# Expert outputs summed in DRAM by accumulating transfers, and another order in the 64-row seats of a mixture of experts

## The chip, the cores and the metric

The kernel runs on one core of a Trainium2 chip, as one program with one launch. The metric is the device time of that launch in microseconds (us), the median of several runs; less is better. Five engines work side by side, each through its own list of instructions: PE (TensorE, matmuls), DVE (VectorE), ACT (ScalarE), POOL (GpSimd) and SP (SyncE, which here only issues transfers). They meet at semaphores.

## The reference

A network of two blocks of layers (gated linear recurrences, attention, convolutional and gated feed-forward layers) over 256 tokens of width 1024 in float32. Only the last layer is touched, a mixture of eight experts of hidden width 3584, two to a token:

```
logits = t @ w_router                        # t: 256 x 1024
top_vals, top_idx = lax.top_k(logits, 2)
gates = softmax(top_vals)
combine = sum(one_hot(top_idx, 8) * gates[..., None], axis=1)
for e in range(8):
    he = (silu(t @ w_gate[e]) * (t @ w_up[e])) @ w_down[e]
    out = out + combine[:, e:e + 1] * he
return rmsnorm(h + out, final_norm)
```

## The kernel before

**Weights.** Every float32 weight matrix comes from DRAM once, in transfers of 1 MB on SP's queue, and each is cut in two pieces of 128 x 1024. ACT writes a rounded copy `hi` of a piece, DVE the rest `lo` (`weights`, `split`, L390 and L391), and PE multiplies with both. Raw weights have twelve buffers in the experts' stage, and `hi` and `lo` four each. A transfer into a raw buffer waits until DVE has read what was in it.

**Seats.** The router (`route`) ranks the experts by how many tokens they got. The rank decides the seat: seats 0, 2, 4 and 6 have 128 rows, seats 1, 3, 5 and 7 have 64. A token row is gathered into a seat by a matmul with a matrix of zeros and ones, `pe` (`expert_picks`, L1804; `expert_gather`), after which ACT and DVE copy the result from PSUM into `xg` (128 rows) or `xgs` (64 rows). In a 128-row seat each product is three matmuls (hi by hi, hi by lo, lo by hi). In a 64-row seat the hi and lo halves of the 64 rows stand side by side in one operand of 128 columns, a product is two matmuls, and the two halves are added afterwards by a matmul with the constant `fold`. One piece of such a seat's up weights, the last, isn't split: PE multiplies it in float32 as it is (`raw`).

**A chunk.** A seat is seven chunks of 512 hidden units (`expert_ffn`). In each PE does the gate product (two 1 MB weights, result `acc`), the up product (two more), and then the down product of the chunk before (`downs`, two weights `w_md`, result `g`). ACT applies Silu to the gate (L1917), DVE multiplies by the up half (L1918, `hc`), PE transposes `hc` into the PSUM tile `pt`, and ACT and DVE write it back as `th`; the next chunk's `downs` need `th`. In a 64-row seat ACT first copies the gate sum (`both`, L1911) and PE folds it.

**Between seats.** At the end of a seat `expert_gate` scales its output by the token's gate on DVE (L1944) and splits it into `y`, hi on ACT and lo on DVE. In chunk 0 of the next seat `expert_scatter` spreads the rows over the 256 tokens by eight matmuls with the transposed `pet`, and DVE adds the four results to the residual `x` (L1957). Seats 1, 3 and 5 also gather the rows of the two next seats, one quarter in each of chunks 2 to 5, and their `pet` and gates in chunk 6 (`hooks`). In `route` the names of the experts and the gates are computed by small DVE instructions (L1755 to L1782) ahead of the first `pe`.

The order of instructions on each engine is that in which the program is written, but where `issue_after` puts one behind another.

Of the kernel before, what the change touches and what calls it, by code (L numbers as in the profile page):

```python
# [21 lines left out]
P = 128  # L22
T = 256
# [11 lines left out]
HALF = P // 2  # L35
PLACE = (0, 4, 1, 5, 2, 6, 3, 7)
# [66 lines left out]
def layout(I):  # L103
# [52 lines left out]
    cst.add("tie", np.tile(np.array([1.0e6] + [-float(e) for e in range(1, 8)], np.float32), (P, 1)))  # L156
    cst.add("fold", (ar[:, None] % HALF == ar[None, :] % HALF).astype(np.float32))
# [83 lines left out]
class Net:  # L241
# [69 lines left out]
    def mm(self, out, lhsT, rhs, start, stop):  # L311
        return self.nc.tensor.matmul(out, lhsT, rhs, start=start, stop=stop)  # L312

    def weights(self, view, raw=None, whole=()):
# [19 lines left out]
        for q in range(pieces):  # L334
# [7 lines left out]
            with ExitStack() as held:  # L342
                if self.hold:
                    for ins in self.hold.pop(0):
                        held.enter_context(self.tc.issue_after(ins))
                self.last_lo = self.split(hi, lo, src)
# [1332 lines left out]
    def route(self, gp, lg, ss, hh, hl, xo):  # L1679
# [33 lines left out]
        with self.tc.issue_after(self.routed.ins):  # L1713
            who, most = self.names(gp, mk, seats, ps[:, 2, :])
            comb = self.gates(mk, S, ss, m, oh1, oh2)
            combp = mk("cp", [P, 2, 8, 2])
            self.seated(gp, seats, combp[:, :, :, 0], comb[:, :, :, 0])
            nc.vector.tensor_copy(combp[:, :, :, 1], comb[:, :, :, 1])
        return hh, hl, xo, posp, combp, (pos, comb, rank, who, most)

    def ranked(self, gp, mk, cnt):
# [10 lines left out]
        seats = self.tl(gp, "seats", S, bufs=1)  # L1732
# [14 lines left out]
    def names(self, gp, mk, seats, cnt):  # L1747
# [5 lines left out]
        who = self.tl(self.rt, "rtwho", [P, 8], I32)  # L1753
        most = self.tl(self.rt, "rtmost", [P, 1], I32)
# [11 lines left out]
        return who, most  # L1766

    def gates(self, mk, S, ss, m, oh1, oh2):
# [9 lines left out]
        comb = mk("cb", [P, 2, 8, 2])  # L1778
# [4 lines left out]
        return comb  # L1783
# [23 lines left out]
    def expert_gather(self, picks, r, q):  # L1807
        nc = self.nc
        pe, xg, kinds = picks
        for part, src in enumerate(r[:2]):  # L1810
            ps = self.tl(self.ps_m, "m", [P, 2, 2, P])
            for c in range(2):
# [5 lines left out]
            for e, small in enumerate(kinds):  # L1818
                if small:
                    sl = slice(HALF * part, HALF * part + HALF)  # L1820
                    dst, src_ = xg[e][:, 2 * q : 2 * q + 2, sl], ps[:, :, e, sl]
                else:
                    dst, src_ = xg[e][:, part, 2 * q : 2 * q + 2, :], ps[:, :, e, :]
                if part == 0:
                    nc.scalar.activation(dst, src_, AF.Copy)
                else:
                    nc.vector.tensor_copy(dst, src_)

    def expert_spread(self, mp, picks, e0, comb):
# [3 lines left out]
        for e in range(len(picks[2])):  # L1833
            ps = self.tl(self.ps_m, "m", [P, 3, P])
            for t in range(2):
                nc.tensor.transpose(ps[:, t, :], pef[:, t, e, :], self.ident)
            for t in range(2):
                self.mm(ps[:, 2, 0:2], pef[:, t, e, :], comb[:, t, e0 + e, :], t == 0, t == 1)
            pet = self.tl(mp, "pet", [P, 2, P], F32R, bufs=4)
            gs = self.tl(mp, "gs", [P, 2], bufs=4)  # L1840
            nc.scalar.activation(pet, ps[:, 0:2, :], AF.Copy)
            nc.vector.tensor_copy(gs, ps[:, 2, 0:2])
            out.append((picks[1][e], pet, gs))
# [9 lines left out]
    def expert_ffn(self, mp, small, first, e, xg, gs, hooks, final):  # L1853
# [5 lines left out]
        def downs(c):  # L1859
            ht = hts.pop(c)  # L1860
            for q in range(2):
                w = self.weights(i["w_md"][e, 2 * c + q])
# [24 lines left out]
        for c in range(7):  # L1887
            gu = []
            for t in range(2):
                ps = self.tl(self.ps_acc, "acc", [P, 512])  # L1890
                for kh in range(2):
# [16 lines left out]
                    if small and (t, kh) == (1, 0):  # L1908
                        both = self.tl(mp, "both", [P, 512], bufs=1)
                        with after(self.last_hi.ins):  # L1910
                            nc.scalar.activation(both, gu[0], AF.Copy)  # L1911
                gu.append(ps)
            if small:
                self.mm(gu[0], self.c("fold"), both, True, True)
            hc = self.tl(mp, "hc", [P, 512])
            with after(self.last_hi.ins):
# [32 lines left out]
    def expert_scatter(self, mp, y, pet, xo, ss=None):  # L1949
        nc = self.nc  # L1950
        for n in range(2):
            for t in range(2):
# [9 lines left out]
    def experts(self, mp, r, out):  # L1962
# [3 lines left out]
        pend = None  # L1966
# [3 lines left out]
        def fetch(e0):  # L1970
            picks = self.expert_picks(mp, e0, r[3], (False, True))
            steps = [lambda q=q: self.expert_gather(picks, r, q) for q in range(4)]
# [144 lines left out]
```

## Time and profile before

| | us |
|---|---|
| median of 3 runs (2133.77 to 2135.83) | 2134.26 |
| the profiled execution | 2133.42 |
| its span, first to last instruction | 2131.6 |
| PE busy in the span | 2025.5 |
| DVE busy | 1771.0 |
| ACT busy | 1389.2 |
| POOL busy | 119.6 |

The profiled execution's time is 1.8 us more than its span. An engine is busy while it executes; register, branch and semaphore instructions don't count, and ends of matmuls are modelled, so that neighbouring matmuls overlap in the rows and their starts tell more than their lengths. The experts begin at about 1143 us and last to the end. Chunks below run from one Silu (L1917) to the next.

### The profile page before, as it was taken

The page shows a single profiled execution, that of the slowest core. Times are in us where ns is not written, and L with a number is a line of the kernel's source. Part 1 is how long each engine was busy: PE and PEld are TensorE (multiplying, and loading weights), DVE is VectorE, ACT ScalarE, POOL GpSimd, SP SyncE. Part 2 cuts the span into 40 slices and gives each one's busy share as a digit, 9 for nine tenths or more (in the row PEclk, how much of TensorE's full clock was granted, in tenths as well). Part 3 has the DMA queues.
Part 4 walks back from the last instruction along what each step waited for, and adds up shares of the span by engine and source line. Part 5 has one row for each costly group of instructions (what it writes and reads, how often), then busy time and mean ns, then how long its engine had stood idle before and what let it go on. Part 6 is the DMA issues. An engine that isn't in the chain of part 4 may idle for free.

```text
span 2131.6 us, 34865 instructions
## 1 busy us (share of the span) xinstructions
PE 2025.5 (95%) x13159; PEld 1744.7 (82%) x13159; DVE 1771.0 (83%) x2896; ACT 1389.2 (65%) x1950; POOL 119.6 (6%) x178
## 2 busy tenths in 40 slices
PE   9999999999999899999887999999989999999997
PEld 8889998889999789999887877778666876678764
DVE  7788888659897679886866989898889988898887
ACT  7566565456556575445535878878777777778785
POOL 1000001002120001222200000000000000000000
PEclk9999999999999999999998999999999999999999
DMA  6335544333654344556564999999999999999992
GB/s 242 131 123 203 178 160 159 104 135 135 219 201 166 87 161 175 210 215 220 204 243 159 360 357 378 396 355 379 342 353 368 368 364 337 360 369 367 349 390 114
DMA packets 80336, 540.13 MB, mean 253 GB/s; under 512 B 9216, under 2 KB 10592, under 8 KB 18208
## 3 DMA queue, kind: packets, MB, share of 16 engines
q1 hardware_dynamic: 76080, 523.59, 65.9%
q0 software_dynamic: 4080, 14.24, 1.8%
q8 instruction: 105, 1.72, 0.3%
q14 instruction: 71, 0.58, 0.1%
HBM read 527.74 MB, written 10.06 MB: 252 GB/s over the span
## 4 chain that ended last, share of the span: by engine, by line
PE 78%; DVE 14%; DMA 3%; issue 2%; ACT 2%; SPq 0%; DVEq 0%; ACTq 0%
PE acc L312 37%; PE g L312 36%; DVE lo L391 6%; PE m L312 4%; DMA raw<-w_me 1%; ACT hi L390 1%; DMA raw<-w_md 1%; PE m L1930 1%; DVE xz L1539 1%; DVE hc L859 1%; PE m L934 0%; DVE y L391 0%; ACT U L1488 0%; PE m L1436 0%; DVE hc L1944 0%
## 5 line engine op out<-in xcount | busy, mean ns | idle before, releaser
L391 DVE TENSOR_TENSOR lo<-raw,hi 128x1024 fp32r<-128x1024 f32 (+1 forms) x956 | 1128.6, 1215 | 185.3 <-ACT hi L390 175.9
L390 ACT ACTIVATE hi<-raw 128x1024 fp32r<-128x1024 f32 (+1 forms) x956 | 983.6, 1051 | 323.7 <-PE g L312 196.9
L312 PE MATMUL g<-xh,hi 128*128 128x256 f32 (+1 forms) x1612 | 462.0, 287 | 14.9 <-ACT xh L467 9.2
L312 PE MATMUL g<-xl,hi 128*128 128x256 f32 (+1 forms) x1612 | 460.8, 286 | 0.8 <-DVE xl L471 0.7
L312 PE MATMUL g<-xh,lo 128*128 128x256 f32 (+1 forms) x1612 | 457.6, 284 | 2.1 <-DVE lo L391 2.1
L312 PEld LDWEIGHTS g<-xh,hi 128*128 128x128 f32 (+1 forms) x1612 | 308.2, 192 | 19.5 <-ACT xh L467 10.8
L312 PEld LDWEIGHTS g<-xh,lo 128*128 128x128 f32 (+1 forms) x1612 | 308.7, 192 | 4.2 <-DVE lo L391 3.4
L312 PEld LDWEIGHTS g<-xl,hi 128*128 128x128 f32 (+1 forms) x1612 | 308.9, 192 | 3.1 <-DVE xl L471 1.5
L312 PE MATMUL acc<-hi,xg 128*128 128x512 f32 x896 | 283.0, 392 | 0.0
L312 PE MATMUL acc<-lo,xgs 128*128 128x512 f32 x392 | 176.5, 450 | 25.4 <-DVE lo L391 24.7
L312 PEld LDWEIGHTS acc<-hi,xg 128*128 128x128 f32 x896 | 168.1, 188 | 35.0
L312 PE MATMUL acc<-lo,xg 128*128 128x512 f32 x448 | 176.3, 394 | 1.8 <-DVE lo L391 1.8
L312 PE MATMUL g<-lo,th 128*128 128x512 f32 x448 | 167.9, 409 | 1.2 <-DVE lo L391 1.2
L312 PE MATMUL g<-hi,th 128*128 128x512 f32 x448 | 159.9, 415 | 1.2 <-ACT th L390 1.2
L312 PE MATMUL acc<-hi,xgs 128*128 128x512 f32 x392 | 154.1, 397 | 0.0
L312 PE MATMUL acc<-ah,lo 128*128 128x256 f32 x528 | 148.0, 281 | 1.4 <-DVE lo L391 1.4
L312 PE MATMUL acc<-al,hi 128*128 128x256 f32 x528 | 148.6, 282 | 0.0
L312 PE MATMUL acc<-ah,hi 128*128 128x256 f32 x528 | 147.2, 282 | 0.0
L312 PEld LDWEIGHTS acc<-lo,xgs 128*128 128x128 f32 x392 | 73.5, 188 | 84.0 <-DVE lo L391 66.9
L312 PEld LDWEIGHTS g<-hi,th 128*128 128x128 f32 x448 | 84.4, 188 | 29.4 <-issue 5.5
L312 PEld LDWEIGHTS acc<-lo,xg 128*128 128x128 f32 x448 | 84.2, 188 | 23.5 <-DVE lo L391 6.2
L312 PEld LDWEIGHTS g<-lo,th 128*128 128x128 f32 x448 | 79.7, 188 | 28.4 <-DVE lo L391 14.2
(512 smaller groups left out, 3019.5 us busy)
## 6 DMA issues: line engine op xcount, KB each, us to landing
raw<-w_me SPq DMA_DIRECT2D x223, 1024.0 KB, 7.0
raw<-w_md SPq DMA_DIRECT2D x112, 1024.0 KB, 7.1
raw<-w_fu SPq DMA_DIRECT2D x44, 1024.0 KB, 4.9
raw<-w_fd SPq DMA_DIRECT2D x22, 1024.0 KB, 4.8
raw<-w_su SPq DMA_DIRECT2D x22, 1024.0 KB, 4.9
raw<-w_ev SPq DMA_DIRECT2D x11, 1024.0 KB, 4.8
raw<-w_sd SPq DMA_DIRECT2D x11, 1024.0 KB, 4.9
raw<-w_oqk SPq DMA_DIRECT2D x8, 1024.0 KB, 4.8
```

The source lines that it names most:

```text
L312: return self.nc.tensor.matmul(out, lhsT, rhs, start=start, stop=stop)
L390: self.last_hi = self.nc.scalar.activation(hi, src, AF.Copy)
L391: return self.nc.vector.tensor_sub(lo, src, hi.bitcast(F32))
L859: nc.vector.scalar_tensor_tensor(hc[:, m, s:], hr[:, m, : T - s], self.g("fcw%d%d" % (l, 2 - s), c), hc[:, m, s:], op0=ALU.mult, op1=ALU.add,)
L1539: nc.vector.tensor_tensor_scan(z[:, ri].rearrange("p j n -> p (j n)"), ro.rearrange("p j n -> p (j n)"), t1[:, ri].rearrange("p j n -> p ( ...
L1930: nc.tensor.transpose(pt[:, b, :], hc[:, b * P : (b + 1) * P], self.ident)
```

## The change

Five parts. (a) For seats 0 to 6 the output isn't split and scattered on chip: ACT scales it straight from PSUM into `yo` (two instructions of 128 x 512), and POOL issues one indirect transfer of 512 KB that adds the 128 rows of `yo` to rows of a DRAM tensor `moesum` (`expert_add`). The tensor has two planes of 384 rows; the row of each is token number or a spare row, computed with the gates (`to`). Seat 7 keeps `expert_gate` and `expert_scatter`, and only it still gets a `pet`. (b) Seat 7 loads the two planes by SP (1 MB each, chunks 2 and 4), and DVE adds each to the residual by two instructions of 128 x 1024 (chunks 3 and 5). (c) In the 64-row seats the down weights are asked for and split ahead of Silu and `hc`; the gather's matmuls follow the gate product; their copies follow `hc`; and the fold precedes the unsplit piece. (d) The names and gates of `route` are written behind the first gather's matmuls. (e) Six transfers of zeros, 512 KB each, fill `moesum`; POOL issues them early in the network, in a stretch that lies at about 138 to 343 us of the trace before.

```diff
+    def expert_add(self, mp, py, gs, to):
+        nc = self.nc
+        y = self.tl(mp, "yo", [P, D], bufs=1)
         for n in range(2):
+            nc.scalar.activation(y[:, 512 * n : 512 * n + 512], py[n], AF.Copy, scale=gs[:, 0:1])
+        nc.gpsimd.indirect_dma_start(
+            out=self.sumd,
+            out_offset=bass.IndirectOffsetOnAxis(ap=to, axis=0),
+            in_=y,
+            in_offset=None,
+            bounds_check=2 * PLANE - 1,
+            compute_op=ALU.add,
+        )
...
@@ expert_ffn
+                    if small and t == kh == 1:
+                        both = self.tl(mp, "both", [P, 512], bufs=1)
+                        with after(self.last_hi.ins):
+                            nc.scalar.activation(both, gu[0], AF.Copy)
                     for k in range(4):
+                        if small and t == kh == 1 and k == 2:
+                            with after(self.last_mm.ins):
+                                self.mm(gu[0], self.c("fold"), both, True, True)
...
-            if small:
-                self.mm(gu[0], self.c("fold"), both, True, True)
+                if t == 0:
+                    with after(self.last_mm.ins):
+                        kept = [hook(small) for hook in hooks.get(c, ())]
+            wd, behind = None, (self.last_hi, self.last_lo)
+            if small and c > 0:
+                wd = [self.weights(i["w_md"][e, 2 * (c - 1) + q]) for q in range(2)]
+                behind = self.past
             hc = self.tl(mp, "hc", [P, 512])
-            with after(self.last_hi.ins):
+            with after(behind[0].ins):
                 nc.scalar.activation(hc, gu[0], AF.Silu, scale=gs[:, 1:2])
-            nc.vector.scalar_tensor_tensor(hc, gu[1], gs[:, 1:2], hc, op0=ALU.mult, op1=ALU.mult)
-            if c in hooks:
-                hooks[c]()
+            with after(behind[1].ins):
+                nc.vector.scalar_tensor_tensor(hc, gu[1], gs[:, 1:2], hc, op0=ALU.mult, op1=ALU.mult)
+            for keep in kept:
+                if keep:
+                    keep()
             if c > 0:
-                downs(c - 1)
+                downs(c - 1, wd)
...
@@ experts
+        def load(plane):
+            t = self.tl(mp, "xg", [P, 2, D], bufs=1)
+            rows = self.sumd[PLANE * plane : PLANE * plane + T]
+            nc.sync.dma_start(t, rows.rearrange("(t p) d -> p t d", p=P))
+            return t
...
+        for step in steps[:-1]:
+            step(False)()
+        with self.tc.issue_after(self.picked.ins):
+            self.rest(mp)
+        steps[-1](False)
...
-            pend = (self.expert_gate(mp, py, gs), pet)
-        self.expert_scatter(mp, pend[0], pend[1], xo, ss)
+            if e < 7:
+                self.expert_add(mp, py, gs, pet)
+        self.expert_scatter(mp, self.expert_gate(mp, py, gs), pet, xo, range(2), ss)
...
@@ mixers
+        zero = n.tl(cp, "zero", [P, D])
+        nc.gpsimd.memset(zero, 0.0)
+        n.sumd = tc.dram_tile([2 * PLANE, D], F32, name="moesum")
+        for b in range(2 * PLANE // P):
+            nc.gpsimd.dma_start(n.sumd[b * P : (b + 1) * P], zero)
```

How the order moves is shown at three places. The first is DVE where the experts begin, before the change: the end of the small instructions for the gates, then the first `pe` and the first `lo` of the experts' weights. The instruction that writes `rtpp`, which is all that `pe` needs, stands 33 rows ahead of `pe`.

```order
L1777 TENSOR_TENSOR rtg_14222<-rtg_14222 128x2
L1779 TENSOR_TENSOR rto_2226_14150<-rto_2226_14150,rtg_14222 128x16
L1780 TENSOR_TENSOR rto_2227_14151<-rto_2227_14151,rtg_14222 128x16
L1781 TENSOR_TENSOR rtcb_14229<-rto_2226_14150,rto_2227_14151 128x16
L1739 TENSOR_TENSOR seat_14235<-seats_14183,rtcb_14229 128x128
L1745 TENSOR_REDUCE rtcp_14234<-seat_14235 128x16
L1804 TENSOR_TENSOR pe_14245<-cstt,rtpp_14187 128x2x128 x2
L391 TENSOR_TENSOR lo_14352<-raw_14349,hi_14351 128x1024
```

The same place of the change, from `rtpp` on (`whot`, `rs_v`, `whof` and what follows are the names and gates).

```order
L1758 TENSOR_REDUCE rtpp_14196<-seat_14197 128x16
L1811 TENSOR_TENSOR pe_14210<-cstt,rtpp_14196 128x2x128 x2
L1766 TENSOR_TENSOR whot_14271<-rtseat_14192,cstt 128x64
L415 TENSOR_SCALAR rs_v_14284<-m_13565 128x2
L1767 TENSOR_REDUCE whof_14272<-whot_14271 128x8
L416 TENSOR_SCALAR rs_s_14287<-rs_v_14284 128x2
```

`pe` has moved up behind `rtpp`; the names and gates follow it, mixed with the gather's copies and `lo` pieces.

The second place is ACT in a chunk of seat 3, before: from the copy for the fold (`both`) to the `th` of that chunk.

```order
L1911 ACTIVATE both_17687<-acc_17628 128x512
L390 ACTIVATE hi_17691<-raw_17689 128x1024
L1917 ACTIVATE hc_17702<-acc_17628,gs_16267 128x512
L390 ACTIVATE hi_17721<-raw_17719 128x1024
L390 ACTIVATE hi_17725<-raw_17719 128x1024
L390 ACTIVATE hi_17739<-raw_17737 128x1024
L390 ACTIVATE hi_17743<-raw_17737 128x1024
L1825 ACTIVATE xg_17409<-m_17837 128x256
L1825 ACTIVATE xgs_17411<-m_17837 128x2x64
L390 ACTIVATE hi_17763<-raw_17761 128x1024
L390 ACTIVATE hi_17767<-raw_17761 128x1024
L390 ACTIVATE th_17771<-m_17755 128x4x64
```

The same stretch of the change.

```order
L1933 ACTIVATE both_17784<-acc_17709 128x512
L395 ACTIVATE hi_17795<-raw_17793 128x1024
L395 ACTIVATE hi_17799<-raw_17793 128x1024
L395 ACTIVATE hi_17805<-raw_17803 128x1024
L395 ACTIVATE hi_17809<-raw_17803 128x1024
L1954 ACTIVATE hc_17813<-acc_17709,gs_16215 128x512
L1840 ACTIVATE xg_17374<-m_17749 128x256
L1840 ACTIVATE xgs_17376<-m_17749 128x2x64
L395 ACTIVATE hi_17844<-raw_17842 128x1024
L395 ACTIVATE hi_17848<-raw_17842 128x1024
L395 ACTIVATE th_17852<-m_17836 128x4x64
L395 ACTIVATE hi_17865<-raw_17863 128x1024
```

The four `hi` of the down weights have moved ahead of Silu (`hc`), the gather's copies (`xg`, `xgs`) right behind it, and the last `hi` of the up weights ahead of `both`.

The third place is PE in the same chunk, before: matmuls of `downs` (`g`), the transposes of `hc`, and the gather (`m<-pe,hth`).

```order
L312 MATMUL g_17413<-hi_17725,th_17639 128x512
L312 MATMUL g_17414<-hi_17725,th_17639 128x512
L312 MATMUL m_17755<-cstt,hc_17702 128x64 x4
L312 MATMUL m_17837<-pe_17408,hth_13553 128x256 x4
L312 MATMUL g_17413<-lo_17726,th_17639 128x512
L312 MATMUL g_17414<-lo_17726,th_17639 128x512
```

In the change the gather stands between the last gate piece (`acc_17709`) and the first up piece (`acc_17759`).

```order
L315 MATMUL acc_17709<-hi_17737,xgs_15435 128x512
L315 MATMUL acc_17709<-lo_17738,xgs_15435 128x512
L315 MATMUL m_17749<-pe_17373,hth_13562 128x256 x4
L315 MATMUL m_17754<-pe_17373,htl_13563 128x256 x4
L315 MATMUL acc_17759<-hi_17762,xgs_15435 128x512
L315 MATMUL acc_17759<-lo_17763,xgs_15435 128x512
```

The gather's eight matmuls now stand together, and `downs` of the change run through without them.

## Rows read from the trace of the kernel before

**Rows 1.** The page, parts 1 and 4: busy time, and the chain that ended last.
```profile
PE 2025.5 (95%) x13159; PEld 1744.7 (82%) x13159; DVE 1771.0 (83%) x2896; ACT 1389.2 (65%) x1950; POOL 119.6 (6%) x178
...
PE 78%; DVE 14%; DMA 3%; issue 2%; ACT 2%; SPq 0%; DVEq 0%; ACTq 0%
```

**Rows 2.** Busy time by stretch: start and end, length, engines, clock, DMA share, GB/s.
```profile
138.00:343.00 205.00, 202.18 (x1664) 199.51 (x1663) 171.91 (x399) 126.61 (x190) 0.23 (x1) 1.00 0.47 166
1326.81:1341.69 14.88, 14.88 (x69) 11.37 (x68) 13.70 (x16) 12.61 (x17) 0.00 (x0) 1.00 1.01 419
1396.76:1642.52 245.76, 233.12 (x1000) 174.02 (x999) 214.71 (x218) 184.85 (x211) 0.00 (x0) 1.00 0.95 358
1426.39:1443.30 16.91, 16.91 (x77) 13.89 (x76) 15.39 (x15) 13.56 (x15) 0.00 (x0) 1.00 0.98 350
1567.61:1585.29 17.68, 15.78 (x67) 10.87 (x66) 14.34 (x16) 12.75 (x16) 0.00 (x0) 1.00 0.93 330
2039.18:2054.82 15.64, 15.21 (x59) 9.68 (x58) 13.72 (x14) 12.34 (x15) 0.00 (x0) 1.00 0.95 376
```

**Rows 3.** Timeline of PE, one chunk of seat 3: start us, us, operation, count.
```profile
1566.55 1.02 PE L312 MATMUL acc<-both,cstt 128*128 128x512 f32 x2
...
1571.22 0.62 PE L312 MATMUL g<-lo,th 128*128 128x512 f32 x2
1571.68 0.64 PE L312 MATMUL g<-hi,th 128*128 128x512 f32 x2
1572.15 1.00 PE L312 MATMUL m<-cstt,hc 128*128 128x64 f32 x8
1572.96 0.72 PE L312 MATMUL m<-pe,hth 128*128 128x256 f32 x4
1573.52 0.62 PE L312 MATMUL g<-lo,th 128*128 128x512 f32 x2
...
1578.14 0.50 PE L312 MATMUL acc<-lo,xgs 128*128 128x512 f32 x1 [1.42 <-DVE lo L391]
...
1580.93 0.50 PE L312 MATMUL acc<-lo,xgs 128*128 128x512 f32 x1 [0.47 <-DVE lo L391]
```

**Rows 4.** Timeline of DVE, the same chunk.
```profile
1576.52 0.42 DVE L1827 CAST xg<-m 128x256 fp32r<-128x256 f32 x1 [1.42 <-PE m L312]
...
1579.66 4.62 DVE L391 TENSOR_TENSOR lo<-raw,hi 128x1024 fp32r<-128x1024 f32 x4
```

**Rows 5.** Timeline of ACT, the same chunk.
```profile
1568.19 3.89 ACT L390 ACTIVATE hi<-raw 128x1024 fp32r<-128x1024 f32 x4
...
1576.05 0.38 ACT L390 ACTIVATE th<-m 128x256 fp32r<-128x256 f32 x1
```

**Rows 6.** Timeline of PE, where seat 3 ends and seat 4 begins.
```profile
1633.91 0.73 PE L312 MATMUL m<-y,pet 128*128 128x512 f32 x2 [1.04 <-ACT y L390]
1635.04 0.50 PE L312 MATMUL acc<-lo,xg 128*128 128x512 f32 x1 [0.40 <-DVE lo L391]
...
1637.37 0.50 PE L312 MATMUL acc<-lo,xg 128*128 128x512 f32 x1 [0.21 <-DVE lo L391]
```

**Rows 7.** Timeline of ACT, the same place.
```profile
1633.22 1.29 ACT L390 ACTIVATE y<-hc 128x512 fp32r<-128x512 f32 x2 [2.10 <-DVE hc L1944]
```

**Rows 8.** Timeline of DVE, start of the experts.
```profile
1142.91 0.28 DVE L1745 TENSOR_REDUCE rtpp<-seat 128x16 f32<-128x128 f32 x1
...
1147.91 0.75 DVE L1804 TENSOR_TENSOR pe<-cstt,rtpp 128x256 fp32r<-128x256 f32 x2
```

**Rows 9.** Timeline of PE, start of the experts.
```profile
1148.71 1.23 PE L312 MATMUL m<-pe,hth 128*128 128x256 f32 x4 [7.90 <-DVE pe L1804]
```

**Rows 10.** Waits of the DMA queue of SP, seats 2 and 3: total us, times, longest.
```profile
SPq L330 <- DVE lo L391: 177.6, 82, 6.3
```

**Rows 11.** DMA issues, whole span: operation, count, KB each, us to landing.
```profile
s5fd<-hp POOLq DMA_DIRECT2D x8, 512.0 KB, 3.7
...
et<-s5et POOLq DMA_DIRECT2D x8, 512.0 KB, 6.2
```

More of the change, by code (lines that the diff above doesn't have):

```diff
@@ L156, in layout @@
     cst.add("tie", np.tile(np.array([1.0e6] + [-float(e) for e in range(1, 8)], np.float32), (P, 1)))
+    cst.add("token", (np.arange(2)[None, :] * P + ar[:, None] - T).astype(np.float32))
+    cst.add("row", np.stack([T + ar, T + ar % HALF + PLANE * (ar // HALF)], axis=1).astype(np.float32))
     cst.add("fold", (ar[:, None] % HALF == ar[None, :] % HALF).astype(np.float32))
@@ L311, in mm @@
     def mm(self, out, lhsT, rhs, start, stop):
-        return self.nc.tensor.matmul(out, lhsT, rhs, start=start, stop=stop)
+        self.last_mm = self.nc.tensor.matmul(out, lhsT, rhs, start=start, stop=stop)
+        return self.last_mm
     def weights(self, view, raw=None, whole=()):
@@ L1745, in seated, with names @@
         return self.nc.vector.tensor_reduce(out, t, axis=AX.X, op=ALU.add)
-    def names(self, gp, mk, seats, cnt):
+    def names(self, gp, who, most, seats, cnt):
         nc = self.nc
@@ L1805, in expert_picks, with expert_gather @@
         return pe[:, :, 0:n, :], xg, kinds
-    def expert_gather(self, picks, r, q):
+    def expert_gather(self, picks, r, q, late=False):
         nc = self.nc
         pe, xg, kinds = picks
-        for part, src in enumerate(r[:2]):
+        pss = []
+        for src in r[:2]:
             ps = self.tl(self.ps_m, "m", [P, 2, 2, P])
+            pss.append(ps)
             for c in range(2):
@@ L1817, in expert_gather, with keep, expert_spread @@
                     )
-            for e, small in enumerate(kinds):
-                if small:
[L1820 to L1829, printed above, removed]
+        def keep():
+            for part, ps in enumerate(pss):
+                for e, small in enumerate(kinds):
+                    if small:
+                        sl = slice(HALF * part, HALF * part + HALF)
+                        dst, src_ = xg[e][:, 2 * q : 2 * q + 2, sl], ps[:, :, e, sl]
+                    else:
+                        dst, src_ = xg[e][:, part, 2 * q : 2 * q + 2, :], ps[:, :, e, :]
+                    with ExitStack() as held:
+                        if late:
+                            held.enter_context(self.tc.issue_after((self.last_hi, self.last_lo)[part].ins))
+                        if part == 0:
+                            nc.scalar.activation(dst, src_, AF.Copy)
+                        else:
+                            nc.vector.tensor_copy(dst, src_)
+        return keep
+    def expert_spread(self, mp, picks, e0, comb, late=False, last=True):
         nc = self.nc
@@ L1832, in expert_spread @@
         out = []
-        for e in range(len(picks[2])):
+        n = comb.shape[-1]
+        for e, small in enumerate(picks[2]):
             ps = self.tl(self.ps_m, "m", [P, 3, P])
+            if last:
+                for t in range(2):
+                    nc.tensor.transpose(ps[:, t, :], pef[:, t, e, :], self.ident)
             for t in range(2):
[L1836 to L1843, printed above, removed]
+                self.mm(ps[:, 2, 0:n], pef[:, t, e, :], comb[:, t, e0 + e, :], t == 0, t == 1)
+            gs = self.tl(mp, "gs", [P, 3], bufs=4)
+            with ExitStack() as held:
+                if late:
+                    held.enter_context(self.tc.issue_after(self.last_hi.ins))
+                    held.enter_context(self.tc.issue_after(self.last_lo.ins))
+                nc.vector.tensor_copy(gs[:, 0:n], ps[:, 2, 0:n])
+                if last:
+                    to = self.tl(mp, "pet", [P, 2, P], F32R, bufs=1)
+                    nc.scalar.activation(to, ps[:, 0:2, :], AF.Copy)
+                else:
+                    to = self.tl(mp, "to", [P, 1], I32, bufs=4)
+                    k = 1 if small else 0
+                    nc.vector.tensor_tensor(gs[:, 2:3], gs[:, 2:3], self.c("row")[:, k : k + 1], op=ALU.add)
+                    nc.vector.tensor_copy(to, gs[:, 2:3])
+            out.append((picks[1][e], to, gs))
         return out
@@ L1857, in expert_ffn, with downs @@
         hts = {}
-        def downs(c):
+        def downs(c, wd=None):
             ht = hts.pop(c)
             for q in range(2):
-                w = self.weights(i["w_md"][e, 2 * c + q])
+                w = wd[q] if wd else self.weights(i["w_md"][e, 2 * c + q])
                 order = [(kk, n) for kk in range(2) for n in range(2)]
@@ L1971, in fetch, with spread, add @@
             picks = self.expert_picks(mp, e0, r[3], (False, True))
-            steps = [lambda q=q: self.expert_gather(picks, r, q) for q in range(4)]
-            return steps + [lambda: queue.extend(self.expert_spread(mp, picks, e0, r[4]))]
+            steps = [lambda late, q=q: self.expert_gather(picks, r, q, late) for q in range(4)]
+            def spread(late):
+                for b in range(2):
+                    part = (picks[0][:, :, b : b + 1, :], picks[1][b : b + 1], picks[2][b : b + 1])
+                    queue.extend(self.expert_spread(mp, part, e0 + b, r[4], late, e0 + b == 7))
+            return steps + [spread]
+        def load(plane):
[3 more added lines that the diff above has]
+            return t
+        def add(t, n):
+            x = xo[:, :, n, :]
+            nc.vector.tensor_tensor(x, x, t[:, n].rearrange("p (q k) -> p q k", q=4), op=ALU.add)
         def call():
```

57 lines of the change are left out of this document (29 added, 28 removed).

## The prediction

> **What bounds the kernel now.** I read the page first. PE is busy for 2025.5 of the 2131.6 us, and 78% of the chain that ended last is PE, 14% DVE, 3% transfers [rows 1]. An average over the whole network says little about a change that touches only the experts, so next I read busy time by stretch [rows 2]. Over seats 2 and 3, from 1396.76 to 1642.52, PE has 233.12 us of work in 245.76. The 12.6 us that it stands are not spread evenly: a chunk of a 128-row seat (1426.39 to 1443.30) has PE busy for all of its 16.91 us, one of a 64-row seat with a gather (1567.61 to 1585.29) for 15.78 of 17.68. One without a gather, in seat 7, takes 15.64. So the 128-row chunks are bound by PE, which the change leaves as it is there, and what can be won lies in the 64-row seats and between the seats.
>
> In the 64-row chunk DVE has 14.34 us and ACT 12.75, so neither is full; it must be an order that makes PE wait. The timelines show it. PE stands 1.42 us at 1578.14 and 0.47 at 1580.93, for a `lo` piece of the gate's weights [rows 3]. DVE itself stood 1.42 us at 1576.52, with the gather's copy at the head of its list and the gather's matmuls still scattered among PE's `downs` [rows 4]; behind that copy stood the `lo` pieces. It is a loop through PE, DVE and PE.
>
> The transfers I looked at last. Their share is 0.95 over the two seats at 358 GB/s, but SP's queue waits 177.6 of these 245.8 us for DVE, which has yet to read a raw buffer [rows 10]. A transfer thus starts when a buffer comes free. In seat 1, where buffers came free faster, 419 GB/s were moved at a share of 1.01 [rows 2]. I take 419 as what the transfers can do.
>
> **The order in 64-row seats.** The durations come from starts of neighbours, since ends are modelled. A down or gate matmul steps 0.23 us (1571.22 to 1571.68 is two); the transposes take 0.81 (1572.15 to 1572.96); four gather matmuls 0.56, so eight 1.1. From the fold's start at 1566.55 to 1571.22 PE does the fold, seven matmuls of up pieces, the unsplit piece and two down matmuls; less nine steps of 0.23, fold and unsplit piece take 2.6 [rows 3]. A `lo` steps 4.62 / 4 = 1.155 [rows 4], a `hi` 3.89 / 4 = 0.97, and `th` takes 0.38 [rows 5].
>
> Three floors for a chunk of the change: PE's own list is 16 gate, 12 up and 16 down matmuls, 44 x 0.23 = 10.1, with 2.6, 0.81 and 1.1: 14.6 us. DVE's is 14.34. The transfers' is 6 x 1.049 MB / 419 GB/s = 15.0. The order adds a loop. In the new rows of ACT, `th` stands ahead of the `hi` of the last gate weights, and PE has `downs` run through, then the transposes, then needs that gate piece. So: downs 3.68, transposes 0.81, `th` 0.38, one `hi` 0.97, two `lo` 2.31, what is left of the gate piece after its first matmul 0.69, gather 1.1, three up pieces 2.76, fold and unsplit piece 2.6: 15.3. I add 0.1 for hand-overs, a choice, and take **15.4**, above all three floors. The down weights' four `hi` and four `lo` lie beside the up matmuls and the fold, which is the time in which PE waited for nothing before either.
>
> Against 17.7 this is -2.3 us. Seats 3 and 5 have four such chunks each: 8 x -2.3 = **-18.4**. Seat 1 gets nothing from it: its chunk of 14.88 is already under 15.4 [rows 2], since it starts with buffers full. Bounds: -3.1 per chunk (PE's floor), so -24.8, and 0 if another wait takes the loop's place.
>
> **Between the seats.** Where a 128-row seat follows, PE stands 1.04 us for `y`, then 0.40 and 0.21 for `lo` pieces that are late behind `y` [rows 6]. The scatter itself is eight matmuls, 8 x 0.23 = 1.84. All of it lies on PE, which is the bound there: 3.5 us, three times, **-10.5**. ACT and DVE lose the split of `y` (1.29 us on ACT, after 2.10 of idling for DVE) and get two scaled copies of the same size on ACT; I cost them at 1.29 [rows 7], hidden, because PE goes on with the next seat's gate, whose first pieces are split by then. If that cover were missing, it would be 1.3 per seat. Where a 64-row seat follows (four times) the same 1.84 us of matmuls go, but there PE isn't the bound in the first chunks; between 0 and -3.5 I take -1.5 each, **-6**.
>
> POOL gets seven indirect transfers of 512 KB. No row shows one. The nearest are POOL's plain writes of 512 KB, which land in 3.7 us, and reads, 6.2 [rows 11]. Added up, as for a read followed by a write, an add would hold the engines 9.9 us at most; by bytes alone, 1.05 MB at 419 GB/s, 2.5. Nothing waits for its landing but the next use of `yo`, a seat (over 110 us) later, and the plane loads. What it can cost is the engines' time. A pair of seats moves 84 MB-sized weights, 88.1 MB, 210 us at 419 GB/s; the change would have the pair take 245.8 - 9.2 - 3.5 - 1.5 = 231.6. So 21 us per pair are free, over 10 per add: both bounds are covered, and I take 0. The zero fills lie in a stretch with a DMA share of 0.47, PE busy for 202.18 of 205 us and POOL for 0.23 [rows 2]; 6 x 3.7 = 22 us of transfers fit in it. I take 0, and 3 as the other end.
>
> **The start.** `pe` needs `rtpp`, which starts at 1142.91, but DVE comes to it only at 1147.91 [rows 8], and PE has stood 7.90 us [rows 9]. The new order puts `pe` behind `rtpp`: 4.7 us earlier. The small instructions aren't gone; they stand among the gather's copies and the first `lo`, of which some wait for them. I take **-3.5**, with 0 and -4.7 as ends.
>
> **Seat 7.** Four adds of 128 x 1024 on DVE, like a `lo` each, 4.6 us, and 2.1 MB more to move, 5 us at 419 GB/s. The new order without a gather could give 15.4 - 1.1 = 14.3, but DVE's list is then 13.72 [rows 2] + 1.15 and the transfers' floor 15.0, against 15.64 now. I take +0.5, between -5 (five chunks at 14.7) and +5 (adds and loads wholly in the way). SP's plane loads wait for seat 6's add, and weights queue behind them; the twelve raw buffers, two chunks of work, stand between.
>
> **Sum.** -18.4 - 10.5 - 6 - 3.5 + 0.5 = -37.9. The profiled execution took 2133.4, so 2095.5; the median of the runs is 0.8 above it: **2096**.
>
> **A page's rule beside the row.** Rows 2 show 419 GB/s with a share of 1.01. The Trainium skill, "SBUF — State Buffer", section "Summary: rules for kernel authors", says to reckon transfers between HBM and SBUF at about 358 GB/s, since HBM binds. The two seats' mean is just 358, which by that rule would be the limit and not the demand. The trace disagrees for 15 us of seat 1; what it would make of the time is the second rival.
>
> **Rivals.**
> *An accumulating transfer is dear.* If its rows are read and written one after the other, it may hold the sixteen engines far longer than 9.9 us. From about 10 us on every further us delays the weights, seven times over: slower than before by 0.2% from 10 + (38 + 4.3) / 7 = 16 us of all engines per add. At 20 us the time is 2096 + 70 = 2166. For it: no row has such a transfer. Against: the bound of 9.9.
> *The transfers' limit is the two seats' mean, 358 GB/s.* Then a pair needs 88.1 MB and two adds of 1.05, 90.2 MB, 252 us against 245.8 now: +6.2 for three pairs and a half, and the planes 5.9: +28, about 2162. For it: the share of 0.95 and the even mean. Against: 419 in seat 1, and SP's queue, which waits for buffers 72% of the time.
> *The order gives a part.* ACT's longer run ahead of Silu, or the gather's hold on PSUM, makes a new wait, and 64-row chunks come to 16.5 to 17. Then -8 in place of -18.4, and with half of the seat boundaries -20 in all: 2114. For it: DVE has 14.34 of 15.4, little room.
> *No change.* The weights' supply sets the pace of the pair, so that only the start is won and the planes take it back: 2134.
>
> **Chances.** The forecast (between 2080 and 2106) 0.60; a part (2106 to 2130) 0.25; no change 0.05; dear adds 0.06; the limit of 358 GB/s 0.04. 0.2%, 4.3 us, is about what a measurement of this kernel can tell from no change. So faster 0.85, same 0.05, slower 0.10. The range must leave out no more than 0.2: below, all the ends together (-24.8, -10.5, -14, -4.7, -5) aren't likely; 2080 is -53. Above, 2122 takes in most of the partial case. That leaves out 0.15 of the slower and unchanged cases and a few hundredths of the partial one.
>
> **What would show it.** In the profile after: Silu to Silu in seats 3 and 5 at 15.4 (right) or over 16.5 (wrong), with PE's wait for `lo` in the gate the only one left. At seat ends no idle time of PE for `y`, and the scatter's matmuls in none but seat 7. The first gather's matmul about 4.7 us after the last router matmul's result, not 7.9. GB/s in small chunks at 400 or more; if it stays at 360 with ACT waiting for weights, the second rival holds. The adds' issue to landing, and whether SP's waits on DVE turn into waits of ACT for transfers, tells the first.

## The result

The changed kernel takes 2101.16 us (median of 4 runs, 2097.26 to 2104.37) against 2135.05: ratio 0.9844, 95% interval 0.9829 to 0.9858, 33.9 us less. The forecast was 2096 in 2080 to 2122. The profiled execution took 2097.96, its span 2096.1, 35.5 less than before. The median lies 5 us above the forecast: 2.5 of it is what the sum of the forecast misses in the trace, the rest is that the median lies 3.2 above the profiled execution, where the forecast had put 0.8. Its page, busy time and chain [rows 1]:

```profile
PE 2000.8 (95%) x13089; PEld 1738.3 (83%) x13089; DVE 1740.6 (83%) x2859; ACT 1382.9 (66%) x1943; POOL 135.3 (6%) x192
...
PE 79%; DVE 11%; ACT 4%; DMA 4%; issue 2%; SPq 0%; ACTq 0%; DVEq 0%
```

PE has 24.7 us less to do, and what it stood has shrunk as well. Busy time by stretch, columns as in [rows 2]: the zero fills' stretch, seats 2 and 3 (Silu to Silu), a 128-row chunk, a 64-row chunk with a gather, and one chunk of seat 7.

```profile
138.00:343.00 205.00, 202.17 (x1664) 199.53 (x1663) 171.90 (x398) 126.56 (x190) 4.58 (x8) 1.00 0.51 181
1386.38:1619.16 232.78, 225.81 (x980) 172.21 (x979) 204.93 (x206) 183.04 (x209) 3.08 (x2) 1.00 0.98 384
1415.03:1431.97 16.94, 16.94 (x78) 13.92 (x77) 15.06 (x15) 13.59 (x16) 0.00 (x0) 1.00 0.99 368
1566.90:1582.55 15.65, 15.10 (x67) 11.08 (x66) 14.28 (x17) 12.50 (x18) 0.00 (x0) 1.00 0.98 402
1985.60:2002.77 17.17, 14.42 (x58) 9.72 (x57) 15.58 (x15) 12.40 (x15) 0.00 (x0) 1.00 1.01 418
```

Seats 2 and 3 take 232.78 in place of 245.76. The 128-row chunk is what it was (16.94 against 16.91 in [rows 2]), the 64-row chunk 15.65 in place of 17.68, and the transfers move 402 GB/s in it. In the zero fills' stretch PE has the same 202.17 of 205 us, at a DMA share of 0.51 against 0.47. A chunk of seat 7 takes 17.17 and has PE stand for 2.75 us.

PE's timeline, at five places: the router's matmuls with the first gather; the last down matmul of seat 2; a chunk of seat 3; seat 3's end with seat 4's beginning; and seat 7.

```profile
1140.43 0.19 PE L315 MATMUL g<-rtsb,onesb 128*128 128x8 bf16 x2 [2.61 <-DVE rtsb L1704]
...
1143.90 1.22 PE L315 MATMUL m<-pe,hth 128*128 128x256 f32 x4 [3.20 <-DVE pe L1811]
...
1498.51 0.39 PE L315 MATMUL g<-hi,tl 128*128 128x512 f32 x1
...
1572.16 1.00 PE L315 MATMUL m<-cstt,hc 128*128 128x64 f32 x8
...
1575.84 0.50 PE L315 MATMUL acc<-lo,xgs 128*128 128x512 f32 x1 [0.55 <-DVE lo L396]
...
1577.78 0.63 PE L315 MATMUL m<-pe,hth 128*128 128x256 f32 x4
1578.25 0.63 PE L315 MATMUL m<-pe,htl 128*128 128x256 f32 x4
1578.72 0.40 PE L315 MATMUL acc<-hi,xgs 128*128 128x512 f32 x1
...
1581.49 1.02 PE L315 MATMUL acc<-both,cstt 128*128 128x512 f32 x2
1582.35 1.88 PE L315 MATMUL acc<-raw,xgs 128*128 128x512 f32 x4
1583.66 0.80 PE L315 MATMUL g<-hi,th 128*128 128x512 f32 x1
...
1610.48 0.39 PE L315 MATMUL g<-lo,th 128*128 128x512 f32 x1
...
1612.71 0.49 PE L315 MATMUL acc<-hi,xg 128*128 128x512 f32 x1 [0.41 <-ACT hi L395]
1613.97 0.50 PE L315 MATMUL acc<-lo,xg 128*128 128x512 f32 x1 [0.76 <-DVE lo L396]
...
1998.65 0.50 PE L315 MATMUL acc<-lo,xgs 128*128 128x512 f32 x1 [2.19 <-DVE lo L396]
```

In the chunk of seat 3 PE waits once, 0.55 us for a `lo` of the gate (1575.84); the gather's eight matmuls stand together from 1577.78 to 1578.72, fold and unsplit piece follow each other, and the downs begin. Before there were two waits, 1.42 and 0.47 [rows 3]. The chain behind the remaining one is seen in DVE's timeline, and in ACT's:

```profile
1142.77 0.29 DVE L1758 TENSOR_REDUCE rtpp<-seat 128x16 f32<-128x128 f32 x1
1143.09 0.76 DVE L1811 TENSOR_TENSOR pe<-cstt,rtpp 128x256 fp32r<-128x256 f32 x2
...
1570.41 2.36 DVE L396 TENSOR_TENSOR lo<-raw,hi 128x1024 fp32r<-128x1024 f32 x2
1573.61 0.42 DVE L396 TENSOR_TENSOR th<-m,th 128x256 fp32r<-128x256 f32 x1 [0.84 <-ACT th L395]
1574.56 10.30 DVE L396 TENSOR_TENSOR lo<-raw,hi 128x1024 fp32r<-128x1024 f32 x9 [0.52 <-ACT hi L395]
...
1593.95 0.16 DVE L1863 COPY gs<-m 128x3 f32<-128x3 f32 x1 [0.26 <-PE m L315]
...
1595.68 0.14 DVE L1871 CAST to<-gs 128x1 int32<-128x1 f32 x1
...
1995.11 2.35 DVE L2041 TENSOR_TENSOR x<-x,xg 128x1024 f32<-128x1024 f32 x2
1997.38 8.03 DVE L396 TENSOR_TENSOR lo<-raw,hi 128x1024 fp32r<-128x1024 f32 x7
2005.33 0.74 DVE L1956 SCALAR_TENSOR_TENSOR hc<-acc,gs,hc 128x512 f32<-128x512 f32 x1
```

```profile
1573.19 0.39 ACT L395 ACTIVATE th<-m 128x256 fp32r<-128x256 f32 x1 [1.87 <-PE m L315]
...
1610.45 1.27 ACT L1992 ACTIVATE yo<-g,gs 128x512 f32<-128x512 f32 x2 [1.25 <-PE g L315]
```

ACT waits 1.87 us for the transposes before `th`; DVE waits 0.84 for `th` and 0.52 for the `hi` behind it. That is the loop that the prediction summed to 15.3 to 15.4; with its 15.6 to 15.65 the trace puts it 0.2 higher.

To place the difference I measure each seat from the last down matmul of the seat before to its own last one; rows 1498.51 and 1610.48 above are the marks of seat 3 (where a row groups several matmuls, 0.23 is added for each step, which makes a mark good to some 0.3 us). The first stretch begins at the router's last matmuls (`g<-rtsb,onesb`). Such marks don't depend on where Silu stands within a chunk, which the change moves by some 2 us. Profiled executions, us; the columns from order_only on are the experiments below:

| to the end of seat | before | after | order_only | adds_only | gates_first | better | th_late | better_th |
|---|---|---|---|---|---|---|---|---|
| 0 (128 rows) | 136.6 | 131.6 | 132.7 | 134.7 | 134.5 | 131.6 | 132.2 | 131.6 |
| 1 (64) | 109.2 | 105.8 | 108.7 | 108.4 | 105.3 | 104.7 | 103.6 | 102.3 |
| 2 (128) | 123.6 | 120.8 | 123.0 | 120.1 | 119.8 | 121.1 | 120.8 | 121.1 |
| 3 (64) | 122.3 | 112.0 | 114.9 | 120.0 | 111.5 | 111.0 | 106.7 | 105.3 |
| 4 (128) | 123.5 | 120.8 | 123.0 | 120.1 | 119.8 | 121.1 | 120.8 | 121.2 |
| 5 (64) | 122.0 | 111.5 | 114.6 | 119.2 | 111.2 | 110.6 | 106.3 | 105.3 |
| 6 (128) | 123.6 | 120.8 | 123.0 | 120.1 | 119.8 | 120.8 | 120.8 | 120.8 |
| 7 (64) | 113.3 | 115.6 | 112.6 | 112.5 | 116.8 | 110.0 | 108.1 | 103.8 |
| end of span | 17.1 | 16.9 | 17.1 | 17.0 | 17.2 | 17.5 | 17.5 | 17.7 |
| sum | 991.1 | 955.7 | 969.6 | 972.1 | 956.0 | 948.3 | 936.6 | 928.9 |

Two cautions in reading it. First, the 128-row chunks of seats 2, 4 and 6 take 16.8 us in gates_first and adds_only (a seat 119.8 to 120.1), and 16.94 to 16.95 in the changed kernel, better, th_late and better_th (120.8 to 121.2), all at a granted clock of 1.00 and with PE busy throughout. Gate and up matmuls follow each other at the same distance in both (three in 0.68 us); most of the difference lies among the down matmuls. Here are the first of the sixteen behind the transposes and the gate matmul after them, in the changed kernel and then in gates_first:

```profile
1421.53 0.48 PE L315 MATMUL g<-lo,th 128*128 128x512 f32 x1
...
1425.36 0.39 PE L315 MATMUL acc<-hi,xg 128*128 128x512 f32 x1
```

```profile
1429.41 0.48 PE L315 MATMUL g<-lo,th 128*128 128x512 f32 x1
...
1433.17 0.39 PE L315 MATMUL acc<-hi,xg 128*128 128x512 f32 x1
```

That is 3.83 and 3.76 us. Both kernels with the shorter chunk have the DRAM sum and the gates ahead of the first gather; the kernel before has the gates there without the sum and takes 16.95, and a second profile of the changed kernel takes 16.94 again. So the shorter chunk may come with the program and not with the execution; why, no run shows. Second, the layers ahead of the experts vary by nearly 8 us (the router's matmul came between 1138.4 and 1146.1), and a run's time goes with its mean granted clock (0.985 at 2097.96, 0.980 at 2104.36); runs of one kernel spread by 2 to 10 us. The traces are therefore compared from the router on.

### The profile page after: what moved, and what is told of

Its sections match the earlier page's. It is cut to its first block, busy times and chain, and to the rows that moved or that the text cites. A ratio compares the mean times of both kernels' runs of the same rounds, so it can differ in the third digit from the quotient of the medians.

```text
span 2096.1 us, 34799 instructions
## 1 busy us (share of the span) xinstructions
PE 2000.8 (95%) x13089; PEld 1738.3 (83%) x13089; DVE 1740.6 (83%) x2859; ACT 1382.9 (66%) x1943; POOL 135.3 (6%) x192
## 4 chain that ended last, share of the span: by engine, by line
PE 79%; DVE 11%; ACT 4%; DMA 4%; issue 2%; SPq 0%; ACTq 0%; DVEq 0%
PE acc L315 38%; PE g L315 36%; DVE lo L396 5%; PE m L315 4%; DMA raw<-w_me 2%; ACT hi L395 2%; DVE xz L1544 1%; DVE hc L864 1%; PE m L1969 1%; PE m L939 1%; ACT U L1493 0%; PE m L1441 0%; DMA raw<-w_md 0%; DVE xl L476 0%; DMA qa<-qpe 0%
## 5 line engine op out<-in xcount | busy, mean ns | idle before, releaser
L315 PE MATMUL acc<-lo,xgs 128*128 128x512 f32 x392 | 164.8, 420 | 19.7 <-DVE lo L396 19.1
L315 PE MATMUL g<-hi,th 128*128 128x512 f32 x448 | 170.1, 419 | 4.9 <-DVE th L396 3.7
L315 PEld LDWEIGHTS g<-lo,th 128*128 128x128 f32 x448 | 84.3, 188 | 25.5 <-DVE lo L396 4.9
```

The source lines that it names most:

```text
L315: self.last_mm = self.nc.tensor.matmul(out, lhsT, rhs, start=start, stop=stop)
```

## The experiments

Theory: the parts of the sum are separate and add up, with the 64-row order as the largest, set by the loop through `th`; the accumulating transfers cost nothing because the transfers have room. Rivals: the order pays only without the scatter; the adds take back what they give; transfers limit the pair.

**The order without the DRAM sum.** `expert_gate` and `expert_scatter` for all seats, no `moesum`:

```diff
-            if e < 7:
-                self.expert_add(mp, py, gs, pet)
+            pend = (self.expert_gate(mp, py, gs), pet)
...
+            if pend is not None:
+                hooks[0].append(lambda late, p=pend: (lambda: self.expert_scatter(mp, p[0], p[1], xo, range(2))))
```

> The changed order in the 64-row seats and the gates behind the first gather stay; outputs are split and scattered on chip as before, with no DRAM sum, no zero fills, no plane loads. My theory (the parts of the sum add up): the eight gather chunks of seats 3 and 5 at 15.4 to 15.7 us, the start 3 to 5 us shorter, the seat boundaries as before: 2135 - 18 - 4 = about 2112 (2108 to 2117). Rival (the order pays only because the scatter is gone from the seats' first chunks): chunks stay near 17 and the time above 2125.

Measured: 2112.25 us (ratio 0.9887, 0.987 to 0.9903). Seats 3 and 5 are 7.4 us shorter than before, with the scatter still in place; 128-row seats gain some 0.5. The rival falls. Which of the moves in part (c) breaks the old loop was not taken apart.

**The DRAM sum on the old order.** The kernel before with `expert_add`, zero fills, plane loads and adds:

```diff
-            pend = (self.expert_gate(mp, py, gs), pet)
-        self.expert_scatter(mp, pend[0], pend[1], xo, ss)
+            if e < 7:
+                self.expert_add(mp, py, gs, pet)
+        self.expert_scatter(mp, self.expert_gate(mp, py, gs), pet, xo, range(2), ss)
```

> The kernel before with the DRAM sum alone: expert outputs scaled on ACT, accumulated by POOL's transfers, zero fills and plane loads; the old order in the 64-row seats and the gates ahead of the first gather. My theory: what lies between the seats goes, about -3.5 us at each of three ends of 64-row seats, -1 to -1.5 at each of the others, and +2 for the loads and adds in seat 7: about 2121 (2117 to 2126), chunks of seats 3 and 5 still at 17.7. Rival (transfers are near their limit, so that the adds' traffic takes back what the scatter gives): 2130 or more.

Measured: 2116.33 us (0.9907, 0.9891 to 0.9924), a little better than expected; its profile is one with the shorter 128-row chunk. Seats 3 and 5 gain 2.3 and 2.8, seats 1 and 7 0.8 each, 128-row seats behind the first 3.4 to 3.5, about 1 of which is the shorter chunk. From the router on the order alone takes 21.5 us less (991.1 - 969.6) and this kernel 19.0 less, 40.5 together, where both at once take 35.4 less; the medians give 43.1 against 33.9. Some 5 us of the excess is the shorter chunk (0.15 in each of the seven chunks of a 128-row seat, and a little in the others). So the two gains add up only if the shorter chunk doesn't come with the DRAM sum in the old order, which no run shows. By seats they add up in 3 and 5, where the largest term lies: 9.7 and 10.2 against 10.3 and 10.5. Elsewhere they don't: seat 1 gains 1.3 by the two apart and 3.4 by both at once, and seat 7 gains 0.7 and 0.8 apart but loses 2.3 by both at once.

**The gates ahead of the first gather again.**

```diff
-        self.rest = rest
+        with self.tc.issue_after(self.routed.ins):
+            rest(gp)
```

> The changed kernel with the names and gates ahead of the first gather again. My theory: the first gather's matmul comes 4 to 5 us later and nothing behind it makes that up, so 2 to 5 us more than the changed kernel: about 2104 (2101 to 2107) where the changed one's lower runs gave 2097. Rival (the small instructions cost as much among the first lo pieces as ahead of them): no difference.

Measured: 2099.83 us (0.983, 0.9814 to 0.9847), under the 2101 to 2107 expected; by the medians the rival, no difference, holds. The trace shows more. From the router's matmul to the gather's first, PE's timeline of this kernel:

```profile
1145.95 0.19 PE L315 MATMUL g<-rtsb,onesb 128*128 128x8 bf16 x2 [2.61 <-DVE rtsb L1704]
...
1154.13 1.22 PE L315 MATMUL m<-pe,hth 128*128 128x256 f32 x4 [7.90 <-DVE pe L1812]
```

That is 8.2 us, against 3.5 in the changed kernel (1140.43 to 1143.90), and the stretch to the end of seat 0 is 2.9 longer, 4 when 1 us is allowed for the shorter chunks. Up to there the small instructions do pay where they stand now. Over the experts as a whole they don't show: from the router on gates_first takes 956.0 us and the changed kernel 955.7 (958.0 in its second profile), because the 128-row chunks of gates_first are shorter. If that comes with the old place of the gates, this part of the change gains nothing in all; that is open.

**What an add costs.** Four more adds behind each, to a second tensor; and the same seven transfers without the addition:

```diff
+        for _ in range(4):
+            nc.gpsimd.indirect_dma_start(
+                out=self.sum2,
...
+                compute_op=ALU.add,
+            )
```

> The changed kernel, and after each add four more adds of the same 512 KB to a second DRAM tensor that nothing reads (with six more zero fills). It prices an add. In the changed kernel's trace the seven adds took 2.3% of the engines' time over 940 us, 3.1 us of all engines each. My theory: 4 x 3.1 = 12 more per seat stay within or just above the 10 us per add that the transfers have free: 0 to 8 us more than the changed kernel (2097 to 2107). Rival (the transfers have no such room, and an add is dear): each extra add costs its 3.1 us or more, 28 x 3.1 = 87 us, about 2185.

Measured: 2104.48 us (0.9855, 0.9838 to 0.9871), 28 more adds for 3.3 us by the medians and 5.0 by the spans (2.7 from the router on, against the second profile of the changed kernel). First the changed kernel's adds: their instructions and landing, and the share of the engines that POOL's queue took from 1160 us on (share in the last column).

```profile
L1993 POOL DMA_INDIRECT moesum<-yo,to x7: 1537/1544/1683, 1273.5 to 1965.1; - x7
...
DMA to landing us min/median/max: 6.1/10.0/10.6
```

```profile
q0 software_dynamic: 1008, 3.67, 2.3%
```

The same queue with 35 adds, and ACT's waits for transfers in it, from seat 5 on (total us, times, longest):

```profile
q0 software_dynamic: 5040, 18.35, 9.8%
```

```profile
ACT hi L395 <- DMA raw<-w_md: 10.4, 12, 2.3
ACT hi L395 <- DMA raw<-w_me: 9.6, 8, 2.8
```

9.8% of 940 us is 92 us for 35 adds, 2.6 each; of the 73 us that the extra ones take, at least 68 were free. Ahead of seat 5 ACT waits for no weights in this kernel. An add is far from the 16 us at which the first rival would have decided.

```diff
-            compute_op=ALU.add,
```

> The changed kernel with the seven indirect transfers writing instead of adding, so that the seats' outputs overwrite each other in DRAM; the sum is left out. Theory (an add's read is covered): as the changed kernel, within 3 us, with a shorter landing than 10 us. Rival (the read and write of each row hold the weights up): faster by 5 us or more.

Measured: 2099.49 us (0.9838, 0.9822 to 0.9853), no different from the changed kernel, as expected, though each transfer is issued and lands sooner:

```profile
L1993 POOL DMA_INDIRECT moesum<-yo,to x7: 972/972/1097, 1272.7 to 1964.4; - x7
...
DMA to landing us min/median/max: 4.9/8.1/9.0
```

**The changed kernel again, and two edits to it.** In chunk 6 of seats 1, 3 and 5 the copies of gates and indices (1593.95 and 1595.68 above, in seat 3) stand in the middle of DVE's `lo` pieces; and in seat 7 the two adds of a plane came together (1995.11 above), ahead of seven `lo`, while PE waited 2.19 us (1998.65). These adds are written behind `hc` of chunk 3, but stand ahead even of `hc` of chunk 2 (2005.33): the order of instructions is not only that of the text, as the section on the kernel before had it; what nothing pins is moved. The first edit, in `expert_spread`, and the second, in `experts`:

```diff
+            def keep(ps=ps, gs=gs, to=to, small=small):
...
+            keeps.append(keep)
...
+                return (lambda: [keep() for keep in held]) if late else None
```

```diff
-                for plane in range(2):
-                    hold = {}
-                    hooks[2 + 2 * plane].append(lambda late, h=hold, p=plane: h.update(t=load(p)))
+            if e >= 6:
+                hold = {}
+                hooks[2].append(lambda late, h=hold, p=7 - e: h.update(t=load(p)))
+                for n in range(2):
+                    hooks[(3, 5)[n]].append(lambda late, h=hold, n=n: lambda: add(h["t"], n))
...
+            with self.tc.issue_after(self.last_lo.ins):
```

> The changed kernel unchanged, for a comparison on one chip with the three that follow, and to see where its own runs differ (2097 and 2104 so far, at mean clocks of 0.985 and 0.981). Theory: the spread comes from clock dips in the layers ahead of the experts, 2097 to 2105 again, and the experts' own part, from the router's last matmul to the end, repeats within 1 us but for PE's step. Rival: the accumulating transfers make the experts' part vary by several us.

> The changed kernel with two edits. The copies of the gates and indices (chunk 6 of seats 1, 3 and 5) go behind hc, as the gather's copies do; and plane 1, which only 64-row seats add to, is loaded and added in seat 6, where DVE has 1.5 us free per chunk, so that seat 7 adds only plane 0, one half in chunk 3 and one in chunk 5. Theory: chunk 6 of seats 1, 3 and 5 falls from 17.1 to 17.7 to 15.6 (-5 us in all, of which half may return at the seat's end), the long chunks of seat 7 (17.2 and 18.5) to 15.6 to 16.5 (-3): 4 to 6 us under the changed kernel. Rival (the waits only move): no difference.

> The changed kernel with the first of those two edits alone: the copies of the gates and indices behind hc. Theory: chunk 6 of seats 1, 3 and 5 at 15.6 in place of 17.1 to 17.7, half of it given back where the next seat begins: 1 to 4 us under the changed kernel. Rival: the seat's end is bound by the gather's last copies anyway, no difference.

> The changed kernel with plane 1 loaded and added in seat 6 and plane 0 in two parts in seat 7, and nothing else. Theory: the two long chunks of seat 7 (17.2 and 18.5 us) fall to 15.3 and seat 6 stays as it is, 4 to 6 us under the changed kernel; with the 3 of spread_late this is all that 'better' won. Rival (seat 6's DVE has no room): seat 6 longer by 2 us, half the gain.

Measured, on one chip: changed again 2100.96 (2097.74 to 2105.98), both edits 2091.45 (0.9795, 0.9781 to 0.9808), gate copies alone 2096.99 (0.9831, 0.9817 to 0.9845). On another chip, planes alone 2092.44 (0.9811, 0.9796 to 0.9826). Both edits together thus gain 9.5 us, more than the 4 to 6 expected.

By the traces, seat 7 falls from 115.6 (116.8 in the run again) to 110.0 with both edits and 109.9 with the planes' alone, and seat 6 stays at 120.8, so its DVE had room. The gate copies bring 1.0 in each of seats 1, 3 and 5 and take 0.3 back in seats 2 and 4, 2.3 in all; from the router on their kernel takes only 0.4 less than the first profile of the changed kernel, since its seat 7 took 117.1.

The changed kernel's second profile differs from its first by 5.6 us up to the router and by 2.4 from there on, more than the 1 us expected; all but 0.6 of the 2.4 (in seat 0) lies in seat 7 and behind it, the seat with the plane loads and adds. Whether they cause it was not tried.

**The loop.** The strongest test of the chunk's length: let `th` follow the last two gate pieces.

```diff
-                    if pend is not None:
+                    if pend is not None and (not small or kh == 1):
                         with after(self.last_lo.ins), after(self.last_hi.ins):
                             turned(*pend)
```

> The changed kernel with one line altered: in the 64-row seats th is written behind the hi and lo of the last two gate pieces, not ahead of them. It breaks the loop that the prediction gave as the 64-row chunk's length (downs, transposes, th, hi, two lo, last gate piece). Theory: chunks of seats 3 and 5 fall from 15.6 to between the transfers' floor of 15.0 and PE's of 14.6, and seat 7's by as much: 8 to 15 us under the changed kernel's 2097 to 2101. Rival 1 (DVE's own list or the transfers hold the chunk at 15.6 already): no difference. Rival 2 (th now comes late for the downs): slower.

> The run 'better' (gate copies behind hc, plane 1 added in seat 6) with the same line altered as in th_late. Theory: its gains and those of th_late add, 2091 less 8 to 15: 2076 to 2083. Rival (the transfers' limit now sets the pace of the pair of seats): no better than th_late, or 128-row chunks longer than 16.95.

Measured: 2079.00 us (0.9751, 0.9734 to 0.9767), and with the two edits **2070.80** (0.9721, 0.9708 to 0.9734), the best version found: 61 us under the kernel before on the same chip, and below the 2076 to 2083 expected. Busy time by stretch of th_late, seats 3 and 4 in part and two chunks of seat 3:

```profile
1518.00:1640.00 122.00, 118.94 (x529) 91.52 (x528) 112.60 (x120) 100.11 (x118) 1.54 (x1) 1.00 1.01 412
1533.11:1547.68 14.57, 14.57 (x67) 11.24 (x66) 14.13 (x16) 12.82 (x18) 0.00 (x0) 1.00 1.01 421
1547.68:1562.24 14.56, 14.56 (x67) 11.24 (x66) 14.12 (x16) 12.81 (x17) 0.00 (x0) 1.00 1.01 418
```

PE is busy for all of 14.57 us: the chunk is at PE's floor, which the prediction put at 14.6, under the transfers' 15.0; that the raw buffers filled in the seat before make up the rest was not tried. From the router on th_late takes 19.1 us less than the changed kernel, more than the 8 to 15 expected: seats 3 and 5 gain 5.3 and 5.2, seat 7, expected to gain as much, 7.5, and seat 1, which the expectation left out, 2.2; better_th takes 26.8 less, the 19.1 and the 7.4 of better together. ACT's timeline of the first of the two chunks:

```profile
1535.52 3.90 ACT L395 ACTIVATE hi<-raw 128x1024 fp32r<-128x1024 f32 x4 [1.28 <-PE g L315]
1539.40 0.39 ACT L395 ACTIVATE th<-m 128x256 fp32r<-128x256 f32 x1
```

`th` now follows four `hi` without a wait, where ACT had waited 1.87 for it. The transfers move 412 GB/s over 122 us and up to 421 within a chunk.

## Why the prediction was right

The forecast of -37.9 stands against -35.4 from the router on in the trace. The terms were less exact than that: seats 0 and 1 gained 3.4 more than forecast, while the 128-row seats behind them, seats 3 and 5, and seat 7 gained 6.1 less, and that the errors cancel is luck. By its steps:

- **The order in 64-row seats, -18.4 and -1.5 for each seat's beginning.** For seats 3 and 5 that is -10.7 each; measured -10.3 and -10.5. The loop was named rightly: undone by one moved instruction, the chunk fell to PE's floor. Its length was 15.6, not 15.4, and chunk 6, which the sum left out, grew by 0.6 and 1.5 (from one Silu to the next), because the gates' copies were in the way.
- **"Seat 1 gets nothing": mis-sized.** With the -1.5 for its beginning the sum gave -1.5; measured -3.4. Neither the order alone (-0.5) nor the DRAM sum alone (-0.8) has it; why the two together gain more stays open.
- **Where a 128-row seat follows, -3.5 each.** Measured -2.8, -2.7, -2.8. The cover of the scaled copies was not whole: ACT's two `yo` stand behind the last down matmul (1610.45, after 1.25 of waiting) and ahead of the next `hi`, so PE still stands 0.41 and 0.76 us (1612.71, 1613.97), where before it stood 1.65 in all [rows 6]. The prediction took these waits as gone.
- **The start, -3.5: a little small.** The stretch to the end of seat 0 fell by 5.0 (4.4 in the second profile); gates_first puts 3 to 4 of it on the gates. The first gather comes 3.5 us after the router's matmul, 4.7 sooner than before. The sign in the prediction, "about 4.7 us after the last router matmul's result", mixed this gain up with the time: PE's wait of 7.90 less 4.7 is 3.2, and 3.20 is what it waits (1143.90).
- **Seat 7, +0.5 and -1.5: mis-sized.** Measured +2.3, 3.3 off, the largest miss. The four adds lie in PE's way, two at a time, the case that the prediction had only as its upper bound: the two chunks with adds take 17.2 and 18.5 us, those without 15.3 to 15.6. With the adds taken apart in planes_apart the seat falls by 5.7, to 3.4 under the kernel before.
- **The adds, 0.** Right. They hold the engines for 2.6 to 3.1 us, near the bound by bytes of 2.5. That they land in 10.0 us, about the 9.9 that a write and a read of 512 KB add up to, is chance: the prediction gave 9.9 as a bound on the engines' time, and beside the weights the write alone lands in 8.1, not 3.7. The zero fills, 0: PE's work in their stretch is 202.17 us, and 202.16 in order_only, which has none.
- **The first rival** (dear adds) falls with adds_x5; **the second** with th_late: 358 GB/s was what the kernel before asked for, and 412 are moved for 122 us. The Trainium skill, "SBUF — State Buffer", section "Summary: rules for kernel authors", says to use about 358 GB/s for HBM to SBUF; this core's trace does not bear that out, and the measurement decides. SP's queue still waits for DVE in the changed kernel, 156.6 of 233 us in seats 2 and 3, against 177.6 of 245.8 [rows 10]:

```profile
SPq L334 <- DVE lo L396: 156.6, 73, 4.4
```

What stays open: why the down matmuls are quicker in gates_first and adds_only, and with it what the place of the gates is worth; why seat 1 gains more than by its parts; and how the layers ahead of the experts come to their clock.

## What to carry to other kernels

Where one engine should be the bound and stands, add up the loop of waits that the new order leaves, not only each engine's work: here that sum was right within 0.3 us, and it named the instruction to move next, which gave over half as much again as the change itself. An accumulating transfer from an idle queue was a cheap place for a sum here, where nothing waited for its landing and the transfers' mean lay under their best stretch. And what a change brings back into the engine that feeds the bound, as the plane adds here, belongs in the seats where that engine has room.

## What the runs showed of the hardware

- POOL was occupied for 1.54 us by an indirect accumulating transfer of 512 KB, 0.97 by the same without the addition; landings were 10.0 and 8.1 us beside a full stream of weights.
- 412 GB/s held over 122 us on one core, at a share of 1.01.
- The same sixteen down matmuls of a 128-row chunk took 3.76 us in gates_first and 3.83 in the changed kernel, both at a granted clock of 1.00.
